# Layer 1 of a two-layer transformer: the second key heads' projection moves behind the first query pairs, the attention's slot table opens earlier, and its prologue runs by a finer clock

## The chip, the cores and the metric

The kernel runs on one core of one Trainium2 chip. The metric is the device time of one execution in microseconds. The kernel before takes 3030.74 us, the median of three runs from 3030.3 to 3031.72.

## The reference

A small diffusion transformer with two layers on 1024 latent tokens and 256 context tokens, model width 1024, 16 heads of 64. Layer 0 mixes by neighbourhood attention, layer 1 by full attention over context and latents with 16 query heads that share 4 key and value heads; both have a gated feed-forward part behind them. The part that matters here is layer 1's mixer:

```python
def qknorm_gqa_mixer(h_lat, h_ctx, w_qkv, q_gain, k_gain, w_o, ang_row, ang_col, with_ctx_out):
    ...
    q, k, v = project_qkv(h_lat, w_qkv, GQA_HEADS, GQA_KV_HEADS)
    qc, kc, vc = project_qkv(h_ctx, w_qkv, GQA_HEADS, GQA_KV_HEADS)
    q = axial_rope(rms_norm(q, q_gain), ang_row, ang_col)
    k = axial_rope(rms_norm(k, k_gain), ang_row, ang_col)
    kc = rms_norm(kc, k_gain)
    k_all = jnp.concatenate([kc, k], axis=1)
    v_all = jnp.concatenate([vc, v], axis=1)
    ...
    def block(q_b):
        s = jnp.einsum('bqhgd,bshd->bhgqs', q_b, k_all).astype(jnp.float32) * scale
        p = jax.nn.softmax(s, axis=-1).astype(v_all.dtype)
        return jnp.einsum('bhgqs,bshd->bqhgd', p, v_all)
    ...
```

## The kernel before, in words

All products are float32 made from two parts, a high and a low one, so that each dense product is three matmuls: high by high (L770), low activations (L771) and low weights (L772). A block of a projection is eight such triples for 512 tokens (24 matmuls of 128x512), or for the 256 context tokens (24 of 128x256); the values have their own three lines (L2105 to L2107).

The stage at hand is layer 1's mixer. Its projections are jobs in one queue of a class Lanes (`bg`): values, queries in pairs of heads (q0 to q7, two heads each, in two blocks of 512 tokens), keys in two pairs: K1d[0] serves the heads 0 to 7, K1d[1] (the job "kv2") the heads 8 to 15. Then comes the output projection. `pump(cost)` gives credit, up to a cap, and emits matmul triples of the first job until it is spent; one triple costs 1. A block that is done is handed to a side generator, finish_qk1, which emits its normalisation and rope: a copy out of PSUM by ScalarE (L2153), a square (L2158), a mean over the head by TensorE (L2162), logarithm and exponential (L2166, L2168), a product on VectorE (L2170), a shuffle (L2176), then on GpSimd or VectorE L2178, L2180 and L2182, the high part on ScalarE (L2188) and the low one (L2190), and the writes to DRAM. A weight tile goes through a similar generator: load, high part (L682), low part (L684).

The prologue before the attention can use four PSUM banks for these blocks (bank1: two S, ps1, X) if the job says so (`prolog`), and temporaries from the set `early` or `late`; in the attention there is one bank, ps1, and `late` has two tiles xn and one each of rs, y, ph and pl. `tick()` moves the emission's own clock by 650 ns, offers each engine's slots to the side generators, and pumps 1. `turn()` moves it by 227 ns, serves only engines that it holds to be idle by their estimated busy time, and pumps a third.

The attention is a list of 64 pairs (16 heads, two blocks of 512 queries, two pairs of 128-query tiles in each). A Plan places the steps of each pair by the table ORDER1 (a name and a time within the pair, in ns, at a period of 8172) and sorts them all by time. X and S are scores (X against the context keys, S against the latent ones, each from two K tiles: L2230, L2231, L2246, L2247), m and mX maxima, e exponentials (L849), s the scaling by the sum on GpSimd (L860), T the transposes (L867), c the copies out of PSUM (L875, L880), PV the product with the values (L497), r and z the output (L895, L907, L908). Between them stand background slots, FILL: PF pumps the projection queue by the phase's rate (1.262), AF, DF and GF offer a slot of ScalarE, VectorE or GpSimd to the side generators, MS and LN the mean and the logarithm. The last three periods have slots without a pair; the first has only its own. head_setup1 loads a head's keys, values and queries into SBUF; it first runs `bg.until` for the head's query block, that is, ticks until that block is finished, and for head 8 until "kv2" is. Its keys' tiles take the memory that the prologue's value tiles (`c`) leave.

Of the kernel before, what the change touches and what calls it, by code (L numbers as in the profile page):

```python
# [25 lines left out]
PAIRS = HEADS // 2  # L26
# [5 lines left out]

V_NMIX, V_NFFN, V_NFIN, V_B, V_QG, V_KG, V_C = 0, 16, 32, 40, 136, 137, 138
V_N = 154
CFG = dict(lag=3, tv=8.0, tm=5.0, t1=43.0, t2=58.0, p0=28, lo="GD", n=39, ra=2.3, rc=0.7, rq=1.1, rb=1.05, gap=263, r1=1.262, lh=300, tk='ADAG', tb=1000000000.0, tg=1, lp='GD')
PERIOD1 = 8172
ORDER1 = {
# [35 lines left out]
def _build(tc, nc, I, O, top):  # L73
    v, s, g, t = nc.vector, nc.scalar, nc.gpsimd, nc.tensor

    def dma(out, in_):
        if out.dtype == F32R:
            out = out.bitcast(F32)
        if in_.dtype == F32R:
            in_ = in_.bitcast(F32)  # L80
        nc.sync.dma_start(out=out, in_=in_)
# [17 lines left out]
    def vec(base, k):  # L99
        return vecs[:, base + k:base + k + 1]  # L100
# [127 lines left out]
    K1d = [dram.tile([2, P, LAT + CTX], F32R, name=f"K1d{p}") for p in range(2)]  # L228
# [38 lines left out]
    def startup():  # L267

        ET = mybir.EngineType
        with ExitStack() as ph:  # L270
# [10 lines left out]
            def start(at, gen):  # L281

                heapq.heappush(todo, (at, next(count), gen))
# [9 lines left out]
            def load_raw(k, src):  # L293
                raws[k] = wraw.tile([P, D], F32, name="wr")
                if k[0] == "v":
                    dma(out=raws[k][:].rearrange("p (u n) -> p u n", u=2), in_=src.rearrange("u p n -> p u n"))
                else:
                    dma(out=raws[k][:], in_=src)

            def loads():  # L300
                W = I["wqkv0"]
                for m in range(KC):
                    load_aw(m)
                    yield 2.9
                    if m < 2:
                        load_x(0, m)
                        yield 2.9
                    if m in (2, 4):
                        k = "k" if m == 2 else "q"
                        load_raw(k, W[8 if m == 2 else 0])  # L310
                        start(now + 3.5, split(k, wsp))
                        yield 1.5
                for i in range(2):
                    load_raw(f"v{i}", W[16:18, :, i * 512:i * 512 + 512])
                    start(now + CFG["tv"], split(f"v{i}", w0))
                    yield 1.5
                for i in range(2):
                    load_x(1, i)
                    yield 2.9
                xs.append(tmp.tile([P, KC, 256], F32, name="aw", bufs=3))  # L320
                load_x(2, 0, 1)
                yield 2.9
                for w in range(2):
                    dma(out=Cd[w], in_=crow[w][:])
                    yield 1.5
                for m in (1, 9):
                    load_raw(f"u{m}", W[m])
                    yield 1.5
                for _ in bias_steps():
                    yield 0.7  # L330

            def split(k, pool):
                hi = pool.tile([P, D], F32R, name="wh")
                lo = pool.tile([P, D], F32R, name="wl")
                ws[k] = hi, lo
                s.copy(hi[:], raws[k][:])
                yield 1.2
                v.tensor_tensor(lo[:], raws[k][:], hi[:].bitcast(F32), ALU.subtract)  # L338
# [16 lines left out]
            def stat(b):  # L355
                n = BLK[b][1]
                acc = []
                for kc in range(KC):
# [10 lines left out]
                    yield 0.55  # L369
                yield CFG["tm"] if b == 1 else 2.0  # L370
                ms = psp.tile([P, 512], F32, name="ms")
# [65 lines left out]
            def first_qk(b):  # L437
# [3 lines left out]
                for kc in range(KC):  # L441
                    while (b, kc) not in ready or b == 0 and min(kc + CFG["lag"], KC - 1) not in ready:
                        yield 0.2
# [20 lines left out]

            for at, gen in [(0.0, loads()), (5.0, c_rows()), (10.0, stat(0)), (CFG["t1"], stat(1)), (CFG["t2"], stat(2)), (28.0, projections())] + \
                    [(max(9.5, a), modulation(m)) for m, a in enumerate((7.0, 13.0, 18.7, 23.0, 26.0, 30.4, 33.3, 36.2))]:
# [32 lines left out]
    class Ring:  # L499

        def __init__(self, n):
            self.n, self.k, self.back = n, 0, set()
# [41 lines left out]
    class Lanes:  # L544
# [145 lines left out]
            self.rings[job.dst].give(job.ids[i])  # L690

        def pump(self, cost):
            self.credit = min(self.credit + cost, self.cap)
            while self.main and self.credit > 0:
                job = self.main[0]
                if len(job.ws) < job.need:
                    break
                try:
                    r = next(job.gen)
                except StopIteration:  # L700
                    self.main.pop(0)
                    if job.heir is not None:
                        job.heir.ws, job.heir.ids, job.heir.dst = job.ws, job.ids, job.dst
                    else:
                        for i in range(len(job.ids)):
                            self.release(job, i)
                    continue
                if isinstance(r, float):
                    self.credit -= r
                elif r == "wait":  # L710
                    break
                else:
                    self.enter(job.tag, r, 1500)

        def tick(self, cost=1.0):

            self.now += 650
            for e in "TML" + CFG["tk"]:
                if self.busy.get(e, 0) < self.now + CFG["tg" if e == "G" else "tb"]:
                    self.slot(e)  # L720
# [12 lines left out]
    def unit(name, k):  # L733
        return [lambda raw: dma(out=raw[:], in_=I[name][k])]
# [177 lines left out]
    class Plan:  # L912
# [1 line left out]
        FILL = ("PF0", "PF1", "PF2", "AF0", "AF1", "AF2", "AF3", "DF0", "DF1", "DF2", "DF3",  # L914
                "DF4", "GF0", "GF1", "GF2", "MS", "LN")

        def __init__(self, phases):

            self.steps, t0 = [], 0
            for k, (period, order, pairs, rate, gap) in enumerate(phases):  # L920
                extra = 3 if k == len(phases) - 1 else 0
                for name, at in order.items():
                    for j in range(len(pairs) + extra * (name in self.FILL)):
                        self.steps.append((t0 + at + j * period, name, pairs[j] if j < len(pairs) else None, rate))
                t0 += len(pairs) * period + gap
            self.steps.sort(key=lambda x: x[0])
# [93 lines left out]
    class Ffn:  # L1020
# [208 lines left out]
        def more(self):  # L1229

            self.ring.idle += self.again()
            if self.layer == 0:
                self.raws.idle += self.xrs + self.tmp[3:]
                self.S.idle += self.tmp[:3]
                self.outs.idle += self.Tf
                self.raws.leave(self.early.idle, self.prepared)
            else:
                self.raws.idle += self.xrs
                self.S.idle += self.Tf
                self.outs.idle += self.tmp  # L1240
# [539 lines left out]
    with ExitStack() as ph:  # L1780
# [6 lines left out]
        bg = Lanes(pb)  # L1787
# [239 lines left out]
        for i, job in enumerate(bg.main[:2]):  # L2027
# [4 lines left out]
        pairs = [[Pair0(h, ps, i) for h in range(HEADS) for i in range(3 - ps)] for ps in range(2)]  # L2032
        n = CFG["n"]
        plan = Plan([(PERIODA, ORDERA, pairs[0][:n], CFG["ra"], 0), (PERIODA, ORDERA, pairs[0][n:], CFG["rq"], CFG["gap"]),
                     (PERIODB, ORDERB, pairs[1], CFG["rb"], 0)])
# [23 lines left out]
    kg = vec(V_KG, 0)  # L2059
# [3 lines left out]
    busy_banks = set()  # L2063
# [19 lines left out]
    def proj_qk1(dst, gain, blks, temps=None, prolog=False):  # L2083

        def gen(job):
            for b in blks:
                n = BLK[b][1]
                while b not in normed:
                    yield "wait"
                k, ps = yield from bank(prolog)  # L2090
                yield from dense_steps(ps[:, :n], job.ws[0], *acts[b], n)
                yield finish_qk1(ps, dst, gain, b, temps or late, k)
        return gen
# [46 lines left out]
    late = Counted(xn=2, sq=2, rs=1, y=1, ph=1, pl=1)  # L2140
# [282 lines left out]
    def add_q(p, blks, *opts):  # L2423
        bg.add((p, blks[0]), unit("wqkv1", p), proj_qk1(Q1d[p], lambda: qg[:], blks, *opts))
# [14 lines left out]
    add_q(0, (0,), early, True)  # L2439
    bg.add("kv", unit("wqkv1", 8), proj_qk1(K1d[0], lambda: kg, (0, 1, 2), early, True))  # L2440
    bg.add("kv", halves("wqkv1", 10), proj_v1((4, 5, 6, 7, 8, 9)))
    bg.add("kv2", unit("wqkv1", 9), proj_qk1(K1d[1], lambda: kg, (2, 0, 1), late, True))
    add_q(1, (0,), late, True)
    for p in range(2, PAIRS):
        add_q(p, (0,))
    for p in range(PAIRS):
        add_q(p, (1,))
# [13 lines left out]
    live["open"] = True  # L2461
    bg.lo, bg.cap = CFG["lp"], 6.0
    pairs = [Pair1(h, b) for blk in range(2) for h in range(HEADS) for b in (4 * blk, 4 * blk + 2)]
    plan = Plan([(PERIOD1, ORDER1, pairs, CFG["r1"], 0)])
    while bg.pending("kv", (0, 0), "norm1"):
        bg.tick()
    h0.close()
    pb = l1.enter_context(tc.tile_pool(name="pg", bufs=2, reuse_waits="tile"))
    head_setup1(0, 0)
    bg.lo, bg.cap = "D", 3.0  # L2470
    def more():
        return any(job.tag == (1, 0) for job in bg.main)

    while busy_banks - {("ps1", 0)} or more():
        bg.tick(float(more()))
    bg.enter("o0", out_split(0))
    bg.enter("o1", out_split(1))
    live["att"] = True
# [159 lines left out]
```

## Time and profile before

| what | us |
|---|---|
| median of three runs | 3030.74 |
| profiled execution, its own time | 3030.41 |
| its span in the trace | 3028.6 |
| lowest and highest of the three | 3030.3, 3031.72 |

The page gives each engine's busy time and its share of the span; a matmul's duration in a timeline overlaps the next one's, so that the distance of two starts is the time that one costs. "Granted clock" is the share of full speed that TensorE was given. In a list of waits, "PE X L2230 <- ACT Pt L849" reads: TensorE's instruction of line 2230 stood idle until ScalarE's at line 849 was done. The prediction quotes the lines that it uses.

### The profile page before, as it was taken

Reading aid. Unit: us, or ns where it says so; the run is one execution under the profiler, and the core shown is the slowest. Engines: PE = TensorE matmul, PEld = TensorE weight load, DVE = VectorE, ACT = ScalarE, POOL = GpSimd, SP = SyncE. Lnnn points to the kernel's source line nnn. Section 1 sums busy time; section 2 is a strip of 40 time slices with the busy share of each in tenths; the row PEclk is TensorE's granted clock in tenths of the full one; section 3 lists DMA queues with packets and bytes.
Section 4 is the critical chain, followed back from the end, with each engine's and each line's share of the span. In section 5 each row is a group of like instructions: output and inputs, shape, how many; then the busy total and the mean of one; then the engine's idle time right before and its main releaser. Section 6 shows DMA issues by size and latency. Waiting matters only on the chain.

```text
span 3028.6 us, 50110 instructions
## 1 busy us (share of the span) xinstructions
PE 2917.2 (96%) x16460; PEld 2503.2 (83%) x16460; DVE 2304.4 (76%) x4659; ACT 1621.8 (54%) x3739; POOL 1245.6 (41%) x1109
## 2 busy tenths in 40 slices
PE   7999998899999999999999899999999999999998
PEld 4788997788788888888889788888888878888886
DVE  7588778776698785557777588899887887776776
ACT  4345545766652222224456488898887632333444
POOL 4246556766234451121121256666643344223112
PEclk9999999999999999999999999999999999999999
DMA  7777777787535562239656523333323443224962
GB/s 265 218 228 242 225 223 226 226 233 207 201 129 195 195 225 85 96 127 330 213 190 215 167 86 93 100 102 105 111 73 122 139 139 118 105 105 147 325 216 108
DMA packets 307170, 519.03 MB, mean 171 GB/s; under 512 B 46432, under 2 KB 112096, under 8 KB 305120
## 3 DMA queue, kind: packets, MB, share of 16 engines
q1 hardware_dynamic: 306912, 515.84, 52.6%
q8 instruction: 131, 2.15, 0.3%
q14 instruction: 127, 1.04, 0.1%
HBM read 389.61 MB, written 120.18 MB: 168 GB/s over the span
## 4 chain that ended last, share of the span: by engine, by line
PE 77%; DVE 9%; DMA 5%; ACT 3%; POOL 3%; issue 2%; SPq 1%; DVEq 0%; POOLq 0%; ACTq 0%
PE pf L1461 9%; PE pf L1462 9%; PE pf L1463 9%; PE T L867 5%; PE o L497 5%; PE pf L1711 5%; PE pf L1710 5%; PE pf L1709 5%; PE ps L770 3%; PE ps L771 3%; PE ps L772 3%; DMA K<-Kd 2%; PE S L2246 2%; PE S L2247 2%; DVE pT L880 1%
## 5 line engine op out<-in xcount | busy, mean ns | idle before, releaser
L860 POOL TENSOR_SCALAR Pt<-Pt,rc 128x1280 f32<-128x1280 f32 (+3 forms) x288 | 299.4, 1040 | 389.0 <-ACT pT L875 143.8
L875 ACT CAST pT<-T 128x256 fp32r<-128x256 f32 (+2 forms) x672 | 305.0, 477 | 124.7 <-PE T L867 120.1
L880 DVE TENSOR_TENSOR pT<-T,pT 128x256 fp32r<-128x256 f32 (+2 forms) x672 | 341.7, 534 | 31.2 <-ACT pT L875 30.8
L867 PE MATMUL T<-ident,Pt 128*128 128x128 f32 x1952 | 302.5, 274 | 23.8 <-POOL Pt L860 22.9
L867 PEld LDWEIGHTS T<-ident,Pt 128*128 128x128 f32 x1952 | 235.2, 140 | 79.6 <-POOL Pt L860 35.4
L497 PE MATMUL o<-pT,Vt 128*128 128x256 f32 x1952 | 295.6, 290 | 2.3 <-DVE pT L880 2.2
L770 PE MATMUL ps<-ah,wh 128*128 128x512 f32 (+1 forms) x688 | 261.3, 380 | 5.5 <-ACT ah L432 2.6
L497 PEld LDWEIGHTS o<-pT,Vt 128*128 128x128 f32 x1952 | 254.3, 189 | 9.5 <-DVE pT L880 5.7
L771 PE MATMUL ps<-al,wh 128*128 128x512 f32 (+1 forms) x688 | 251.5, 366 | 5.3 <-POOL al L132 3.6
L849 ACT ACTIVATE Pt<-S,rc 128x512 f32<-128x512 f32 (+2 forms) x384 | 247.4, 654 | 9.6 <-DVE rc L841 6.5
L772 PE MATMUL ps<-ah,wl 128*128 128x512 f32 (+1 forms) x688 | 250.9, 365 | 1.4 <-DVE wl L338 1.4
L2238 DVE TENSOR_REDUCE nm<-S 128x1 f32<-128x512 f32 x256 | 169.6, 682 | 35.8 <-PE S L2247 34.1
L952 POOL TENSOR_TENSOR c<-c,c 128x512 f32<-128x512 f32 (+1 forms) x63 | 92.6, 1472 | 248.7 <-DVE c L955 89.5
L955 DVE TENSOR_TENSOR c<-c,c 128x512 fp32r<-128x512 f32 (+1 forms) x166 | 131.3, 804 | 48.5 <-ACT c L1437 34.6
L849 ACT ACTIVATE Pt<-X,rc 128x256 f32<-128x256 f32 x256 | 125.2, 489 | 65.3 <-DVE rc L841 58.6
L1437 ACT CAST wh<-c 128x512 fp32r<-128x512 f32 x112 | 68.9, 618 | 166.9 <-PE pf L1462 66.8
L895 POOL TENSOR_TENSOR r<-ob 128x256 f32<-128x256 f32 x144 | 123.7, 859 | 65.4 <-ACT ob L889 58.7
L772 PEld LDWEIGHTS ps<-ah,wl 128*128 128x128 f32 x688 | 131.1, 191 | 23.3 <-DVE wl L338 2.1
L771 PEld LDWEIGHTS ps<-al,wh 128*128 128x128 f32 x688 | 132.0, 192 | 18.5 <-POOL al L132 5.2
L770 PEld LDWEIGHTS ps<-ah,wh 128*128 128x128 f32 x688 | 131.5, 191 | 18.6 <-ACT ah L432 2.8
L1461 PE MATMUL pf<-c,wh 128*128 128x512 f32 x376 | 146.5, 390 | 0.0
L1462 PE MATMUL pf<-c,wh 128*128 128x512 f32 x376 | 146.5, 390 | 0.0
(599 smaller groups left out, 9155.3 us busy)
## 6 DMA issues: line engine op xcount, KB each, us to landing
c<-in_fout SPq DMA_DIRECT2D x119, 256.0 KB, 4.0
wr<-in_wqkv SPq DMA_DIRECT2D x53, 512.0 KB, 4.2
wr<-in_adaT SPq DMA_DIRECT2D x96, 256.0 KB, 3.2
c<-in_fin SPq DMA_DIRECT2D x68, 256.0 KB, 2.9
adaw<-in_adaT SPq DMA_DIRECT2D x64, 256.0 KB, 4.0
wr<-in_wo SPq DMA_DIRECT2D x32, 512.0 KB, 4.5
wr<-in_fin SPq DMA_DIRECT2D x58, 256.0 KB, 2.7
K<-Kd SPq DMA_DIRECT2D x64, 224.0 KB, 4.6
```

What stands on the lines that cost most here:

```text
L497: t.matmul(o_ap, lhsT=u.V[:, kb, :], rhs=u.pT[:, i, :], start=i == 0, stop=i == len(u.blocks) - 1)
L770: t.matmul(ps, lhsT=hi[:, c], rhs=ah[:, kc, :n], start=kc == 0, stop=False)
L771: t.matmul(ps, lhsT=hi[:, c], rhs=al[:, kc, :n], start=False, stop=False)
L772: t.matmul(ps, lhsT=lo[:, c], rhs=ah[:, kc, :n], start=False, stop=kc == KC - 1)
L849: s.activation(u.Pt[:, off:off + u.wid[c]], u.S[c], AF.Exp, bias=u.min, scale=u.sign, accum_out=u.rc[:, 3 + c:4 + c])
L860: g.tensor_scalar(Pt, Pt, u.rc[:, 2:3], 1.0, ALU.mult, ALU.mult)
L867: t.transpose(T[:, i * P:(i + 1) * P], u.Pt[:, (i0 + i) * P:(i0 + i + 1) * P], ident[:])
L875: s.copy(u.pT[:, i0:i0 + n, :P], u.T[c])
L880: v.tensor_tensor(u.pT[:, i0:i0 + n, P:], u.T[c], u.pT[:, i0:i0 + n, :P].bitcast(F32), ALU.subtract)
L1461: t.matmul(ps[:], lhsT=r32(hi[:, c]), rhs=bh, start=k == 0, stop=False)
L1462: t.matmul(ps[:], lhsT=r32(hi[:, c]), rhs=bl, start=False, stop=False)
L1463: t.matmul(ps[:], lhsT=r32(lo[:, c]), rhs=bh, start=False, stop=k == 3)
```

## The change

Six edits, all in what sets the order around layer 1's prologue and attention:

1. the job "kv2" goes behind q1 and q2 in the queue, and it and q1 no longer take the prologue's banks (they are given the default, one bank, and the set `late`);
2. the prologue's loop runs `turn()` in place of `tick()`; behind it, a loop that ticked until every bank but one was free and q1 done is replaced by 24 turns;
3. Plan gets a last argument: if it is given, FILL slots of six periods ahead of the first pair, from 1400 ns before the start on, are added without a pair at that rate (4.0);
4. the first two pairs form a phase of their own with rate 3.0;
5. the rate of the other pairs goes from 1.262 to 1.31;
6. a single pump may bring as much credit as its cost, even above the cap of 3.

Below line 917 a line of the kernel before stands 7 lines further down in the changed one (L2162 is L2169 there, L2230 is L2237).

```diff
@@ -32,7 +32,7 @@
 
 V_NMIX, V_NFFN, V_NFIN, V_B, V_QG, V_KG, V_C = 0, 16, 32, 40, 136, 137, 138
 V_N = 154
-CFG = dict(lag=3, tv=8.0, tm=5.0, t1=43.0, t2=58.0, p0=28, lo="GD", n=39, ra=2.3, rc=0.7, rq=1.1, rb=1.05, gap=263, r1=1.262, lh=300, tk='ADAG', tb=1000000000.0, tg=1, lp='GD')
+CFG = dict(lag=3, tv=8.0, tm=5.0, t1=43.0, t2=58.0, p0=28, lo="GD", n=39, ra=2.3, rc=0.7, rq=1.1, rb=1.05, gap=263, r1=1.31, lh=300, tk='ADAG', tb=1000000000.0, tg=1, lp='GD')
 PERIOD1 = 8172
 ORDER1 = {
     "PF0": -1360, "X": -660, "GF0": -582, "S00": 0, "mX": 30, "S10": 868, "m00": 930, "m10": 1550, "mn0": 2370,
@@ -690,7 +690,7 @@
             self.rings[job.dst].give(job.ids[i])
 
         def pump(self, cost):
-            self.credit = min(self.credit + cost, self.cap)
+            self.credit = min(self.credit + cost, max(self.cap, cost))
             while self.main and self.credit > 0:
                 job = self.main[0]
                 if len(job.ws) < job.need:
@@ -914,9 +914,16 @@
         FILL = ("PF0", "PF1", "PF2", "AF0", "AF1", "AF2", "AF3", "DF0", "DF1", "DF2", "DF3",
                 "DF4", "GF0", "GF1", "GF2", "MS", "LN")
 
-        def __init__(self, phases):
+        def __init__(self, phases, ramp=0.0):
+
 
             self.steps, t0 = [], 0
+            period, order, pairs, rate, gap = phases[0]
+            for name in self.FILL if ramp else ():
+                for j in range(-6, 0):
+                    at = order.get(name, -1e9) + j * period
+                    if at >= -1400:
+                        self.steps.append((at, name, None, ramp))
             for k, (period, order, pairs, rate, gap) in enumerate(phases):
                 extra = 3 if k == len(phases) - 1 else 0
                 for name, at in order.items():
@@ -2439,9 +2446,10 @@
     add_q(0, (0,), early, True)
     bg.add("kv", unit("wqkv1", 8), proj_qk1(K1d[0], lambda: kg, (0, 1, 2), early, True))
     bg.add("kv", halves("wqkv1", 10), proj_v1((4, 5, 6, 7, 8, 9)))
-    bg.add("kv2", unit("wqkv1", 9), proj_qk1(K1d[1], lambda: kg, (2, 0, 1), late, True))
-    add_q(1, (0,), late, True)
-    for p in range(2, PAIRS):
+    add_q(1, (0,))
+    add_q(2, (0,))
+    bg.add("kv2", unit("wqkv1", 9), proj_qk1(K1d[1], lambda: kg, (2, 0, 1)))
+    for p in range(3, PAIRS):
         add_q(p, (0,))
     for p in range(PAIRS):
         add_q(p, (1,))
@@ -2461,18 +2469,15 @@
     live["open"] = True
     bg.lo, bg.cap = CFG["lp"], 6.0
     pairs = [Pair1(h, b) for blk in range(2) for h in range(HEADS) for b in (4 * blk, 4 * blk + 2)]
-    plan = Plan([(PERIOD1, ORDER1, pairs, CFG["r1"], 0)])
+    plan = Plan([(PERIOD1, ORDER1, pairs[:2], 3.0, 0), (PERIOD1, ORDER1, pairs[2:], CFG["r1"], 0)], 4.0)
     while bg.pending("kv", (0, 0), "norm1"):
-        bg.tick()
+        bg.turn()
     h0.close()
     pb = l1.enter_context(tc.tile_pool(name="pg", bufs=2, reuse_waits="tile"))
     head_setup1(0, 0)
     bg.lo, bg.cap = "D", 3.0
-    def more():
-        return any(job.tag == (1, 0) for job in bg.main)
-
-    while busy_banks - {("ps1", 0)} or more():
-        bg.tick(float(more()))
+    for _ in range(24):
+        bg.turn()
     bg.enter("o0", out_split(0))
     bg.enter("o1", out_split(1))
     live["att"] = True
```

## The prediction

> **What bounds the kernel now.** I read the page's first part, then the table of stretches around the second layer's projections, then TensorE's waits, then the timeline of TensorE and of SyncE's queue at the first attention step. First the page, with each engine's busy time:
>
> ```profile
> span 3028.6 us, 50110 instructions
> PE 2917.2 (96%) x16460; PEld 2503.2 (83%) x16460; DVE 2304.4 (76%) x4659; ACT 1621.8 (54%) x3739; POOL 1245.6 (41%) x1109
> ```
>
> TensorE is the bound and the change leaves its instructions as many as they were, so only its idle time and its clock can move. The span is 1.81 us under the profiled execution's own 3030.41 us, which is 0.33 us under the median of 3030.74. Next some stretches (columns: stretch, length, busy time of PE, its weight loads, DVE, ACT and POOL, granted clock, DMA share, GB/s):
>
> ```profile
> 1600.00:1650.00 50.00, 48.07 (x385) 46.50 (x384) 44.27 (x74) 33.95 (x62) 4.31 (x3) 1.00 0.70 237
> 1650.00:1700.00 50.00, 47.02 (x305) 41.86 (x304) 26.36 (x46) 22.64 (x47) 13.65 (x13) 1.00 0.39 125
> 1690.00:1700.00 10.00, 10.00 (x86) 10.00 (x85) 2.97 (x7) 2.26 (x5) 0.00 (x0) 1.00 0.52 170
> 1710.00:1715.00 5.00, 5.00 (x24) 4.13 (x23) 0.91 (x2) 2.20 (x5) 0.00 (x0) 1.00 1.02 265
> 1725.00:1743.00 18.00, 11.54 (x49) 7.66 (x49) 13.33 (x27) 10.63 (x29) 5.80 (x4) 0.81 0.52 164
> 1800.00:1900.00 100.00, 99.79 (x664) 87.46 (x663) 86.61 (x203) 89.25 (x234) 65.86 (x59) 1.00 0.38 111
> 2600.00:2700.00 100.00, 100.00 (x443) 82.81 (x442) 71.85 (x97) 31.88 (x53) 28.92 (x21) 1.00 0.31 109
> ```
>
> The running attention (1800 to 1900) is 99.8% full: a projection moved into it is not hidden, it costs its TensorE time. That time is 100/443 = 0.226 us for a 128x512 matmul, and 10/86 = 0.116 us for a 128x256 one. The hole is the attention's opening, 1725 to 1743, with 11.5 of 18 us busy at a clock of 0.81. Its waits, and below them those of the rest of that attention half (wanted: total us, times, longest):
>
> ```profile
> PE S L2246 <- ACT xn L2153: 2.9, 1, 2.9
> PE S L2246 <- ACT Pt L849: 2.6, 2, 1.8
> PE S L772 <- DVE wl L684: 1.3, 1, 1.3
> PE ps L770 <- ACT xn L2153: 1.0, 1, 1.0
> PE T L2162 <- DVE pT L880: 1.0, 1, 1.0
> PE T L867 <- POOL Pt L860: 0.4, 1, 0.4
> PE X L2230 <- ACT Pt L849: 0.4, 1, 0.4
> ...
> PE S L2246 <- DVE pT L880: 3.2, 8, 0.7
> ```
>
> **The opening, step by step.** TensorE's rows from the first matmul behind the values' projection to the first product of weights and values (columns: start, duration, operation, and the idle time before it):
>
> ```profile
> 1700.05 0.28 PE L770 MATMUL S<-ah,wh 128*128 128x256 f32 x1
> 1701.73 0.39 PE L772 MATMUL S<-ah,wl 128*128 128x256 f32 x1 [1.28 <-DVE wl L684]
> ...
> 1725.05 0.28 PE L2230 MATMUL X<-K,Qs 128*128 128x256 f32 x1
> 1729.01 0.80 PE L2246 MATMUL S<-K,Qs 128*128 128x512 f32 x1 [2.85 <-ACT xn L2153]
> 1732.01 0.80 PE L2246 MATMUL S<-K,Qs 128*128 128x512 f32 x1 [1.78 <-ACT Pt L849]
> 1734.74 0.63 PE L772 MATMUL ps<-ah,wl 128*128 128x512 f32 x1
> 1735.79 0.39 PE L2230 MATMUL X<-K,Qs 128*128 128x256 f32 x1 [0.41 <-ACT Pt L849]
> 1736.99 0.44 PE L867 MATMUL T<-ident,Pt 128*128 128x128 f32 x2 [0.45 <-POOL Pt L860]
> 1743.08 1.42 PE L497 MATMUL o<-pT,Vt 128*128 128x256 f32 x10
> ```
>
> The waits sum to 1.28+2.85+1.78+0.41+0.45 = 6.8, and the 0.96 on L880 (the list's 1.0) makes 7.7. Seven matmuls from 1732.01 to 1735.17 took 3.16 us, not 7 x 0.226 = 1.58: 1.6 lost to the clock. The two from 1729.01 lost 0.6. The opening of before thus loses 9.9 us.
>
> Now TensorE's order from the last value matmul (S<-wl at L2107) to the first transposes of attention weights (L867); X and S<-K are scores, ps and S<-ah projections. Before:
>
> ```order
> L2107 MATMUL S<-wl,ah_17871 128x256
> L770 MATMUL S<-ah_17871,wh 128x256
> ...
> L770 MATMUL S<-ah_17390,wh 128x512
> ...
> L2162 MATMUL T<-sq,hones 128x512
> ...
> L770 MATMUL ps_18448<-ah_17390,wh 128x512
> L771 MATMUL ps_18448<-al_17391,wh 128x512
> L772 MATMUL ps_18448<-ah_17390,wl 128x512
> L2230 MATMUL X<-K_18280,Qs 128x256
> L2231 MATMUL X<-K_18281,Qs 128x256
> ```
>
> and after, at the same place:
>
> ```order
> L2114 MATMUL S<-wl,ah_17854 128x256
> L770 MATMUL ps_18295<-ah_17390,wh 128x512
> ...
> L2238 MATMUL X<-K_18279,Qs 128x256
> L2253 MATMUL S<-K_18278,Qs 128x512
> L2254 MATMUL S<-K_18279,Qs 128x512
> L770 MATMUL ps_18352<-ah_17390,wh 128x512
> ...
> L2169 MATMUL T<-sq,hones 128x512
> L2253 MATMUL S<-K_18278,Qs 128x512
> ```
>
> Before X stood 24 matmuls of 0.116 and 81 of 0.226 (21 us, the second key heads and one query pair); now 24 of 0.226 remain, 5.4 us. Behind the first four scores now come 12 projection matmuls, then four scores, then 9 more: 21 x 0.226 = 4.7 us and a mean-square (L2169) fill what was idle. But X needs keys and queries from DRAM. SyncE's queue at that place (start, time on the queue, transfer):
>
> ```profile
> 1701.11 0.36 SPq L81 DMA_DIRECT2D V1d<-c  x1
> 1703.59 2.39 SPq L81 DMA_DIRECT2D K<-K1d  x4
> 1706.70 1.09 SPq L81 DMA_DIRECT2D Qs<-Q1d  x2
> ```
>
> and the landing of two of them (KB each, us from issue to landing):
>
> ```profile
> Qs<-Q1d SPq DMA_DIRECT2D x2, 128.0 KB, 9.1
> V1d<-c SPq DMA_DIRECT2D x1, 256.0 KB, 2.3
> ```
>
> The last V1d write landed at 1701.11+2.3 = 1703.4 and the K loads, whose tile reuses its cells, were issued at 1703.59. The queries landed 9.1 us after 1706.7 to 1707.8, that is 1715.8 to 1716.9: 15.8 to 16.9 us after the values' end. The queue's order, before and after:
>
> ```order
> L81 DMA V1d<-c_17794 128x4x128
> L81 DMA wr<-in_wqkv 128x1024
> L81 DMA K_18280<-K1d_133 64x1280 x2
> L81 DMA K_18281<-K1d_133 64x1280 x2
> L81 DMA Vt<-V1d 128x1280
> L81 DMA Qs<-Q1d_125 64x512 x2
> ```
>
> ```order
> L81 DMA V1d<-c_17792 128x4x128
> L81 DMA wr<-in_wqkv 128x1024 x2
> L81 DMA K_18278<-K1d_133 64x1280 x2
> L81 DMA K_18279<-K1d_133 64x1280 x2
> L81 DMA Vt<-V1d 128x1280
> L81 DMA Qs<-Q1d_125 64x512 x4
> ```
>
> A second weight tile (wr, 512 KB) now stands ahead of the keys; at the 265 GB/s of the full stretch it is 2.0 us. So X waits between 15.8-5.4 = 10.4 and 16.9+2.0-5.4 = 13.5 us; I take 12, where before it waited for nothing. TensorE behind it is in order: nothing else starts. The clock then starts low. The row above needed 3.2 us of work to come back, at a loss of 1.6; I take that (the bounds are 0 and the 2.2 that the old opening lost). The Trainium skill (TensorE: Matmul & The Clock Gate, Part 1: The HAM clock gate) says that the clock halves after an idle window of about 3.4 us and comes back after about 3.4 us of sustained work; here it had halved by the end of an idle stretch of only 2.85 us, and the return agrees. By its figure the loss would be half of 3.4, an estimate of 1.7 in place of 1.6.
>
> Of the inner waits I keep 0.3 at the scores and 0.8 at L880. The new opening loses 12+1.6+0.3+0.8 = 14.7 against 9.9: +4.8. The two 50 us stretches ahead of it idle 1.9+3.0 us; the prologue by the clock puts the weights' low halves ahead of the values' copies, so I give it one 1.2 us wait back (0 to 4.9). Net +3.6, from 0 to +7.
>
> **GpSimd and head 6.** The rope of a key or query block in the attention costs GpSimd four operations, beside the scaling L860 that each transpose group waits for (counts and mean ns in the groups by line):
>
> ```profile
> L860 POOL TENSOR_SCALAR Pt<-Pt,rc 128x1280 f32<-128x1280 f32 x128 | 172.2, 1346 | 228.2 <-ACT pT L875 141.1 <-DVE rc L841 50.3 <-DVE rc L855 18.2
> L2182 POOL TENSOR_TENSOR xn<-xn,y 128x512 f32<-128x512 f32 x16 | 25.8, 1612 | 0.1
> L2180 POOL TENSOR_TENSOR y<-y,rope 128x512 f32<-128x512 f32 x15 | 24.2, 1612 | 0.0
> L2178 POOL TENSOR_TENSOR xn<-xn,rope 128x512 f32<-128x512 f32 x17 | 23.5, 1380 | 38.3 <-DVE y L2176 38.3
> L2190 POOL TENSOR_TENSOR pl<-xn,ph 128x512 fp32r<-128x512 f32 x16 | 22.4, 1399 | 2.9 <-ACT ph L2188 2.9
> ```
>
> A block is 1.38+1.61+1.61+1.40 = 6.0 us of GpSimd. With the second keys queued ahead of the third query pair, head 6 finds its queries unfinished: head_setup1's bg.until runs the background there until they are ready, and pushes out the rest of one block and two whole ones. GpSimd's order between the same two scalings (the 21st and 22nd of the attention), before and after (r is an output, z its sum):
>
> ```order
> L860 TENSOR_SCALAR Pt<-Pt,rc 128x1280
> L2180 TENSOR_TENSOR y<-y,rope 128x512
> L907 TENSOR_TENSOR z<-z,r 64x256
> L908 TENSOR_TENSOR z<-z,r 64x256
> L860 TENSOR_SCALAR Pt<-Pt,rc 128x1280
> ```
>
> ```order
> L860 TENSOR_SCALAR Pt<-Pt,rc 128x1280
> L2197 TENSOR_TENSOR pl<-xn,ph 128x512
> L2185 TENSOR_TENSOR xn<-xn,rope 128x512
> L2187 TENSOR_TENSOR y<-y,rope 128x512
> L2189 TENSOR_TENSOR xn<-xn,y 128x512
> L2197 TENSOR_TENSOR pl<-xn,ph 128x512
> L2185 TENSOR_TENSOR xn<-xn,rope 128x512
> L2187 TENSOR_TENSOR y<-y,rope 128x512
> L2189 TENSOR_TENSOR xn<-xn,y 128x512
> L2185 TENSOR_TENSOR xn<-xn,rope 128x512
> L2197 TENSOR_TENSOR pl<-xn,ph 128x512
> L2187 TENSOR_TENSOR y<-y,rope 128x512
> ```
>
> Eleven rope operations, about 16.4 us, stand where one stood. TensorE meanwhile has 54 projection matmuls, 12.2 us, and its usual pair beside them, so the sum of work nearly balances; but it can't run ahead. Projections have one PSUM bank (ps1) here, freed by an ACT copy into one of two xn tiles, and an xn tile comes free only at L2197 of two blocks earlier. I follow the chain: the first block change waits for a rope tail, ACT's exponentials and the copy (about 2), the second for the mean-square's return, rope and L2197 of the block before (about 3), and the pair behind it for ACT, which stands at the third copy (about 1.5). That makes 6.5 if no link overlaps, 2 if only the copies show; the one block change of before that shows such a wait cost 1.0 (ps L770 on xn). I take 5.
>
> At the second pair a smaller pile of five rope operations (7.6 us) now stands between two scalings, with some 6 us of TensorE work beside it: +2, against the 1.0 and 0.4 of before: +0.6 (-1 to +2). The higher rate r1 leaves three instead of six pairs of the half without a projection to fill them; the 3.2 us at L880 in eight waits are theirs, and half of it goes: -1.5 (-3 to 0). The queries of heads 2 and 3 are now loaded behind z's transfer on SyncE, and the last pairs have fewer fillers: +0.7 (0 to +3). The wider cap of the credit only lets the new rates of 3 and 4 through, and is in the order above.
>
> **Sum.** 3.6+5+0.6-1.5+0.7 = +8.4 on 3030.41, 3038.8; with the 0.33 of the median, 3039.1, say 3039.
>
> **Rivals.** (1) Not slower: the burst at head 6 is hidden, since GpSimd's 16.4 us lie beside 12.2 us of projections and a pair of some 7 us. For it: GpSimd's work has cover by sum, and the one wait of TensorE for GpSimd in the list of the opening is 0.4. Against: one bank, two xn tiles. It decides if the copies come within 0.5 us of the blocks' ends. It takes the 5 away: 3034. (2) Faster: the transfers ahead of X are short. All four K loads and the queries were issued into a full queue; without it a load takes what the small writes take, 2.3 (V1d), so X is ready 7.7+2.3 = 10 us after the values and waits 4.6, not 12. With a clock that stays up (-1.6), the prologue's whole 4.9 us given back (-3.7 more) and head 6's burst hidden, 8.4-7.4-1.6-3.7-5 = -9.3: 3021. Against it: the queue is full by this very set of transfers. (3) Worse: the chain at head 6 is serial for each of three blocks, 3 us apiece as in the second step, 9 in place of 5: +12.4, 3043. It decides if rope, tail and copy of a block run one behind the other with ACT's exponentials between them. (4) That the slots of missing pairs pump nothing is excluded by the order above, where their 12 and 9 matmuls stand.
>
> **How the numbers follow.** A measurement of this kernel can tell about 0.2%, 6.1 us: same is 3024.7 to 3036.8. My forecast (3036 to 3042) has 0.45, rival 3 has 0.17, rival 1 0.28, rival 2 0.10. Of the forecast's own spread 0.06 falls under 3036.8. Slower is 0.45-0.06+0.17 = 0.56, same 0.28+0.06 = 0.34, faster 0.10. The range leaves out rival 2 and the far half of rival 3: 3028 to 3046.
>
> **What would show it.** Right: TensorE idle 10 to 13.5 us ahead of the first X with its releaser a DMA of K or Qs; a clock of about 0.5 for the 3 us behind it; TensorE full between the first scores and the first transposes; at head 6 waits of projections on xn summing to some 5 us. Wrong: an X that waits under 7 us, or head 6 without a wait over 1 us, or new waits of over 3 us in later pairs, which I have not counted.

## The result, and the profile after

The changed kernel takes 3050.96 us (median of seven runs, 3039.59 to 3056.45) against 3030.74 for the one before (seven runs, 3026.97 to 3036.26): a ratio of 1.0059, 95% interval 1.0041 to 1.0077. It is slower, by 12 to 23 us. The forecast had the direction, not the size: 3039 lay 12 us too low, and 3046, the top of the range, 5 us.

The profiled execution of the changed kernel took 3039.59 us, the shortest of the seven, so its own distance to before (9.2 us) is not the result. Up to the values of layer 1 both kernels have the same instructions. The first matmul of the values and the last group of the program, in the profile of before (start and duration first):

```profile
1644.60 0.33 PE L2105 MATMUL S<-wh,ah 128*128 128x256 f32 x1
...
3015.00 1.88 PE L168 MATMUL pf<-o,ones 128*128 128x512 f32 x4
```

and in that of after:

```profile
1636.93 0.34 PE L2112 MATMUL S<-wh,ah 128*128 128x256 f32 x1
...
3024.19 1.88 PE L168 MATMUL pf<-o,ones 128*128 128x512 f32 x4
```

This execution was 7.7 us ahead when the changed part began. From there to the end it took 1387.26 us, where before took 1370.40: the changed part costs 16.9 us, which fits the timed ratio. A second profile of the changed kernel (below) had its first values at 1646.29, so the lead was not the change's doing. In the eleven profiles of the experiments this point lies between 1641.56 and 1651.32 us.

The waits of TensorE from there to the middle of the next stage, after (total us, times, longest):

```profile
PE X L2237 <- DMA Qs<-Q1d: 11.5, 1, 11.5
PE ps L770 <- ACT xn L2160: 5.3, 3, 2.7
PE S L2253 <- ACT Pt L849: 4.7, 3, 3.3
PE T L867 <- POOL Pt L860: 3.2, 4, 1.0
...
PE pf L190 <- DVE c L144: 2.3, 1, 2.3
PE S L2253 <- DVE pT L880: 2.1, 5, 0.7
...
PE X L2237 <- ACT Pt L849: 1.9, 6, 0.4
PE pf L770 <- ACT ah L2277: 1.3, 1, 1.3
PE T L867 <- DVE pT L880: 0.7, 1, 0.7
...
PE S L772 <- DVE wl L684: 0.2, 1, 0.2
```

Rows of before that are needed beside these and are not in the prediction, from the same stretch:

```profile
PE T L867 <- POOL Pt L860: 2.2, 4, 0.7
PE pf L190 <- DVE c L144: 0.7, 1, 0.7
PE ps L770 <- DVE al L2287: 0.8, 1, 0.8
PE S L772 <- DVE wl L684: 2.3, 2, 1.3
```

The old waits of the opening on xn (2.9) are gone, those on wl are down from 2.3 to 0.2, and one on a transfer, 11.5, has come. Two waits of after, 2.6 on L1444 and 1.9 on L2165, are as long in before. TensorE's rows at that place (the last column is the idle time before), and the clock behind it (stretch, length, busy times of PE, its loads, DVE, ACT, POOL, then the clock):

```profile
1710.08 0.55 PE L2237 MATMUL X<-K,Qs 128*128 128x256 f32 x1 [11.46 <-DMA Qs<-Q1d]
```

```profile
1710.00:1713.00 3.00, 2.92 (x9) 2.56 (x10) 1.39 (x2) 0.00 (x0) 0.00 (x0) 0.50 1.03 244
1713.00:1716.00 3.00, 3.00 (x11) 2.35 (x11) 1.46 (x3) 1.96 (x5) 0.00 (x0) 0.72 1.00 230
1716.00:1722.00 6.00, 5.54 (x26) 4.07 (x25) 3.09 (x9) 3.54 (x11) 1.70 (x1) 1.00 0.23 80
```

The wait is where the prediction put it. Behind it 3.0 us at half clock and 3.0 at 0.72 lose 1.5+0.8 = 2.3 us; then TensorE is 5.54/6 full up to the transposes.

At the place that the prediction calls the second pair (by the trace GpSimd's pile of five between the fifth and the sixth scaling, at 1738.24 and 1747.48) stands a wait of another kind than the one forecast. ScalarE, GpSimd and TensorE there, after (start, duration, operation, idle before):

```profile
1741.34 1.59 POOL L2189 TENSOR_TENSOR xn<-xn,y 128x512 f32<-128x512 f32 x1
1742.96 0.62 ACT L2195 CAST ph<-xn 128x512 fp32r<-128x512 f32 x1 [2.69 <-POOL xn L2189]
1743.48 0.68 ACT L849 ACTIVATE Pt<-S,rc 128x512 f32<-128x512 f32 x1
1744.31 0.50 PE L2253 MATMUL S<-K,Qs 128*128 128x512 f32 x1 [3.31 <-ACT Pt L849]
```

and a stretch a little later:

```profile
1745.00:1750.00 5.00, 5.00 (x24) 4.50 (x23) 2.79 (x6) 3.70 (x10) 4.52 (x5) 0.66 0.27 91
```

ScalarE stands 2.69 us at the rope's high part (L2195), which waits for GpSimd's sum (L2189). The exponential L849 is behind it in ScalarE's queue, and TensorE's next scores need the PSUM bank that it reads: 3.31 us. No scaling L860 is late. Then the clock halves for a while: 5 us at 0.66 lose 1.7 more. The Trainium skill (TensorE: Matmul & The Clock Gate, Part 1, Architectural detail) says that ScalarE and VectorE are strict first-in-first-out; these four rows agree.

At head 6, the two block changes and the end of the burst:

```profile
1819.81 0.50 PE L770 MATMUL ps<-ah,wh 128*128 128x512 f32 x1 [1.51 <-ACT xn L2160]
1829.08 0.50 PE L770 MATMUL ps<-ah,wh 128*128 128x512 f32 x1 [2.67 <-ACT xn L2160]
1838.03 0.50 PE L2253 MATMUL S<-K,Qs 128*128 128x512 f32 x1 [0.70 <-ACT Pt L849]
1841.47 0.50 PE L770 MATMUL ps<-ah,wh 128*128 128x512 f32 x1 [1.09 <-ACT xn L2160]
```

That is 6.0 us, at the block changes that the prediction followed (a block change is the first matmul of a new projection block, which needs the one bank free again).

### The profile page after: what moved, and what is told of

It reads as the page before. It is cut to its first block, busy times and chain, and to the rows that moved or that the text cites. A ratio compares the mean times of both kernels' runs of the same rounds, so it can differ in the third digit from the quotient of the medians.

```text
span 3037.8 us, 50121 instructions
## 1 busy us (share of the span) xinstructions
PE 2918.2 (96%) x16460; PEld 2504.8 (82%) x16460; DVE 2297.6 (76%) x4657; ACT 1622.0 (53%) x3739; POOL 1245.7 (41%) x1109
## 5 line engine op out<-in xcount | busy, mean ns | idle before, releaser
L860 POOL TENSOR_SCALAR Pt<-Pt,rc 128x1280 f32<-128x1280 f32 (+3 forms) x288 | 299.2, 1039 | 438.5 <-ACT pT L875 143.8
L880 DVE TENSOR_TENSOR pT<-T,pT 128x256 fp32r<-128x256 f32 (+2 forms) x672 | 342.3, 535 | 32.8 <-ACT pT L875 31.9
L770 PE MATMUL ps<-ah,wh 128*128 128x512 f32 (+1 forms) x720 | 274.5, 381 | 9.1 <-ACT xn L2160 5.3
L771 PE MATMUL ps<-al,wh 128*128 128x512 f32 (+1 forms) x720 | 263.7, 366 | 3.6 <-POOL al L132 2.4
L772 PE MATMUL ps<-ah,wl 128*128 128x512 f32 (+1 forms) x720 | 263.5, 366 | 1.4 <-DVE wl L338 1.4
L849 ACT ACTIVATE Pt<-S,rc 128x512 f32<-128x512 f32 (+2 forms) x384 | 247.7, 656 | 18.4 <-DVE rc L841 15.8
L849 ACT ACTIVATE Pt<-X,rc 128x256 f32<-128x256 f32 x256 | 125.5, 490 | 65.4 <-DVE rc L841 58.6
L1444 ACT CAST wh<-c 128x512 fp32r<-128x512 f32 x112 | 68.8, 618 | 167.5 <-PE pf L1469 63.6
L770 PEld LDWEIGHTS ps<-ah,wh 128*128 128x128 f32 x720 | 138.3, 192 | 23.8 <-ACT xn L2160 6.3
L772 PEld LDWEIGHTS ps<-ah,wl 128*128 128x128 f32 x720 | 137.4, 191 | 24.5 <-DVE wl L338 2.1
L771 PEld LDWEIGHTS ps<-al,wh 128*128 128x128 f32 x720 | 138.5, 192 | 17.6 <-POOL al L132 4.0
```

The source lines that it names most:

```text
L770: t.matmul(ps, lhsT=hi[:, c], rhs=ah[:, kc, :n], start=kc == 0, stop=False)
L771: t.matmul(ps, lhsT=hi[:, c], rhs=al[:, kc, :n], start=False, stop=False)
L772: t.matmul(ps, lhsT=lo[:, c], rhs=ah[:, kc, :n], start=False, stop=kc == KC - 1)
L849: s.activation(u.Pt[:, off:off + u.wid[c]], u.S[c], AF.Exp, bias=u.min, scale=u.sign, accum_out=u.rc[:, 3 + c:4 + c])
L860: g.tensor_scalar(Pt, Pt, u.rc[:, 2:3], 1.0, ALU.mult, ALU.mult)
L880: v.tensor_tensor(u.pT[:, i0:i0 + n, P:], u.T[c], u.pT[:, i0:i0 + n, :P].bitcast(F32), ALU.subtract)
```

## The experiments

Theory: the move of the second key heads costs 17 us, by the cover that X loses and by the two piles of rope work; the rest of the change is about neutral. Rivals: the run-to-run clock behind the new wait makes the result; the second key heads cost more wherever in the attention they stand; the other edits cost by themselves. Ratios are to the kernel before on the same chip, with 95% intervals. "Stretch" is the time from the first matmul of the values to the last group in the profile (before 1370.40, after 1387.26).

### The changed kernel again

No edit.

> The changed kernel itself, once more. Theory: in its first profile the stages ahead of layer 1's projections, whose instructions are the same in both kernels, were 7 us shorter than in the profile of before, by chance of the granted clock; the changed stages cost 17 us: 12 to 13 of wait at the first X, the rest in the piles of rope operations at the second pair and at head 6. So 14 to 20 us above before here, with an X wait of 11 to 12 us and 7 to 8 us of projection waits at head 6. Rival: only 10 us are the changed stages, and what runs have above that is half clock behind the new wait; then this profile shows at least 7 us more of half clock in the opening than the first one did (13.7 us).

3051.42 us, ratio 1.0060 (1.0047 to 1.0073), stretch 1389.46. Its waits that differ from the first profile's, or would have to:

```profile
PE X L2237 <- DMA Qs<-Q1d: 14.0, 1, 14.0
PE ps L770 <- ACT xn L2160: 5.3, 3, 2.7
PE S L2253 <- ACT Pt L849: 4.6, 3, 3.3
```

and the stretches from X on:

```profile
1720.00:1723.00 3.00, 2.52 (x8) 2.26 (x9) 1.13 (x2) 0.00 (x0) 0.00 (x0) 0.50 1.04 231
1723.00:1726.00 3.00, 3.00 (x13) 2.46 (x13) 1.72 (x4) 1.67 (x5) 0.00 (x0) 0.92 1.02 201
```

The waits in the list are the same to 0.1 us, but for L2277 (1.6 for 1.3) and X: 14.0 us, 2.5 more than in the first profile and above my bound of 13.5. The projection waits sum to 5.3, under the 7 to 8 expected. Behind X (at 1720.48) TensorE ran at half clock for 2.5 us and at 0.92 for 3.0, which loses 1.3+0.2 = 1.5, less than the 2.3 of the first time. The rival by the clock falls: the span is 11.6 us longer than the first (3049.4, 3037.8); 9.4 of that lie ahead of the changed part and 2.5 at X.

### The move alone

The kernel before with one edit:

```diff
-    bg.add("kv2", unit("wqkv1", 9), proj_qk1(K1d[1], lambda: kg, (2, 0, 1), late, True))
-    add_q(1, (0,), late, True)
-    for p in range(2, PAIRS):
+    add_q(1, (0,))
+    add_q(2, (0,))
+    bg.add("kv2", unit("wqkv1", 9), proj_qk1(K1d[1], lambda: kg, (2, 0, 1)))
+    for p in range(3, PAIRS):
         add_q(p, (0,))
```

> The kernel before with one edit alone: the second key heads go behind q1 and q2, and both lose the prologue's banks. 24 projection matmuls stand ahead of the first X, none behind it until the first product with the values, and a burst of 57 at head 6. Theory: an X wait of 11 to 12, the 8 us behind X idle as before, 8 at head 6: before +18 to +24, so the move by itself costs as much as the whole change or more. Rival, that the prologue by turns, the slots ahead of the first pair or the higher rates carry a good part: under +12.

3052.27, ratio 1.0072 (1.0058 to 1.0087), that is +18 to +26; stretch 1396.05. From its opening and head 6:

```profile
PE X L2230 <- DMA Qs<-Q1d: 8.7, 1, 8.7
PE ps L770 <- ACT xn L2153: 8.6, 3, 5.0
```

The move by itself costs about what the whole change does. Its X wait is shorter than I expected, its block changes longer: the 8.6 are 1.0 in the opening and two of the three waits on xn at head 6, where with the third (1.1, behind the end of this list) and 0.7 on L849 TensorE stands 9.4 us.

### Everything but the move

The changed kernel with "kv2" and q1 back in front with their banks, in place of the 24 turns the loop on busy_banks and more() with `bg.turn()`:

```diff
...
+    bg.add("kv2", unit("wqkv1", 9), proj_qk1(K1d[1], lambda: kg, (2, 0, 1), late, True))
+    add_q(1, (0,), late, True)
...
-    for _ in range(24):
-        bg.turn()
...
+    while busy_banks - {("ps1", 0)} or more():
         bg.turn()
```

> The changed kernel with the second key heads and q1 back in front with the prologue's banks, and the loop ahead of the attention waiting for them as before, by turns. Theory: the cover of the loads is back, no burst at head 6; the chain behind the first scores has 6 fillers and a mean-square instead of 21 matmuls: before -3 to +3. Rival (prologue by turns or the higher rates cost something by themselves): over 5 us above before.

3036.23, ratio 1.0009 (1.0000 to 1.0019), stretch 1373.99: 3.6 more than before, 13 less than the changed kernel. No wait on a transfer is left in its list of 1690 to 1800 us; new is one of 2.7 on xn. So most of the loss is the move's; the other edits gain nothing.

### More cover ahead of X

```diff
-    for _ in range(24):
+    for _ in range(100):
```

> 100 turns in place of 24 ahead of the attention, nothing else: the order then has q1, q2 and a part of the second key heads ahead of the first X (63 matmuls of 128x512 and 24 of 128x256), the fillers behind it stay, and no burst is left at head 6. Theory: the X wait of 11.6 goes to under 1, the 8 us at head 6 go, about 3 us less at the second pair: 17 below the changed kernel, that is before -3 to +2 us. Rival, that the second key heads cost more in the attention wherever they are put: most of them are still in it, so over 10 us above before.

3034.68, ratio 1.0012 (1.0001 to 1.0022), stretch 1377.39. In the opening:

```profile
PE ps L770 <- ACT xn L2160: 6.4, 4, 3.2
PE S L2253 <- DVE pT L880: 1.2, 2, 0.9
PE S L2253 <- ACT Pt L849: 0.7, 1, 0.7
```

No X wait and no burst, by one number; some 15 of 18 us come back (ratio 1.0060 to 1.0012). The rival's bar, over 10 us above before, is not reached. But the trace has 72 matmuls of 128x512 and 24 of 128x256 ahead of X, more than I had counted: two of the three blocks of the second key heads stand there and only one is left in the attention. What all three would cost there with a full cover ahead of X, this run does not show. What is left are waits at block changes, three ahead of X (1.1, 1.0, 3.2) and one behind it (1.0): ahead of X too, the jobs now have one bank and two xn tiles.

### The prologue's banks for q1 and q2, 120 turns

```diff
-    add_q(1, (0,))
-    add_q(2, (0,))
+    add_q(1, (0,), late, True)
+    add_q(2, (0,), late, True)
...
-    for _ in range(24):
+    for _ in range(120):
```

> The changed kernel with 120 turns ahead of the attention and the prologue's banks for q1 and q2: 96 matmuls of 128x512 and 24 of 128x256 ahead of X, 12 with a mean-square and 9 behind the first scores, no burst at head 6. Theory: no X wait, under 2 us of the 6.4 us of bank waits of the run with 100 turns, the chain behind X filled: before -6 to 0. Rival: the second key heads in one bank keep 4 to 6 us of waits: +1 to +5.

3034.85, ratio 1.0009 (0.9999 to 1.0020), stretch 1372.33. The block changes on xn still wait 5.7 us (two, longest 3.2): the rival's case. Both stand ahead of X, between blocks of the second key heads, which have the one bank.

### q3 ahead of the second key heads

```diff
-    add_q(1, (0,))
-    add_q(2, (0,))
+    for p in (1, 2, 3):
+        add_q(p, (0,))
     bg.add("kv2", unit("wqkv1", 9), proj_qk1(K1d[1], lambda: kg, (2, 0, 1)))
-    for p in range(3, PAIRS):
+    for p in range(4, PAIRS):
```

> The changed kernel with q3 ahead of the second key heads too. The opening is the same, the burst of 54 projection matmuls at head 6 is gone, and one of 39 stands at head 8. Theory: the X wait stays 11 to 12; head 6 gives 8 us back, head 8 takes about 5: before +11 to +16. Rival (clock behind the X wait is the cost): as the changed kernel, before +15 to +20.

3055.15, ratio 1.0075 (1.0063 to 1.0088), that is +19 to +27; stretch 1391.48. It is no better than the changed kernel (1.0047 to 1.0073), against both expectations. Waits before and after 1800 us:

```profile
PE X L2237 <- DMA Qs<-Q1d: 12.3, 1, 12.3
...
PE ps L770 <- DVE al L2294: 6.7, 1, 6.7
PE S L2253 <- DVE pT L880: 4.6, 10, 0.8
PE ps L770 <- ACT xn L2160: 1.7, 1, 1.7
```

The waits on xn fell from 5.3 to 2.8 (this 1.7 and 1.1 in the opening), as the theory of head 6 has it; the 1.7 and 0.7 on L849 belong to a burst of 39 projection matmuls at head 8, half of the 5 that I had given it. But a wait of 6.7 us came at the end. The addition L2294, which frees the bank, stands in VectorE's order behind L2279, and that waits for the last heads' results to come back from DRAM, with no other projection queued. That the work pulled forward is what is missing there fits, but no run here separates it.

### The rope's tail on VectorE too

```diff
-            yield "D" if tp is early else "G" if live["att"] else "GD"
+            yield "D" if tp is early else "G" if live["att"] and not bg.pending("kv2") else "GD"
```

> The changed kernel in which the last three rope operations of a block may go to VectorE too, as long as the second key heads are not done (in the attention they are GpSimd's alone). Theory: at the second pair and at head 6 ScalarE stands in order behind GpSimd's rope chain, and TensorE behind ScalarE; with a shorter chain 4 to 8 of these 11 us go: before +10 to +15, the X wait stays. Rival, that the single bank and the two xn tiles alone make the waits at head 6: no change from the changed kernel, before +16 to +20.

3046.69, ratio 1.0046 (1.0032 to 1.0061): some 4 us less than the changed kernel's second measurement, the intervals overlapping; stretch 1389.65, no shorter.

```profile
PE X L2237 <- DMA K<-K1d: 14.0, 1, 14.0
PE ps L770 <- ACT xn L2160: 6.0, 4, 3.3
PE S L2253 <- ACT Pt L849: 1.3, 2, 0.7
```

The four waits on xn, one by one:

```profile
1750.46 0.59 PE L770 MATMUL ps<-ah,wh 128*128 128x512 f32 x1 [3.27 <-ACT xn L2160]
1829.26 0.50 PE L770 MATMUL ps<-ah,wh 128*128 128x512 f32 x1 [0.98 <-ACT xn L2160]
1836.63 0.50 PE L770 MATMUL ps<-ah,wh 128*128 128x512 f32 x1 [0.76 <-ACT xn L2160]
1848.91 0.50 PE L770 MATMUL ps<-ah,wh 128*128 128x512 f32 x1 [1.01 <-ACT xn L2160]
```

The waits of scores on L849 fell from 4.7 to 1.3 (1.9 with one behind 1850 us), longest 0.7 (3.3 in the changed kernel): the second pair's wait was ScalarE behind GpSimd's rope. But nothing is won there, since a block change at the same place now waits 3.3 on its xn tile. At head 6 the three waits on xn fell from 5.3 to 2.8, and 0.7 on L849 stays: of the 6.0 us there, GpSimd's rope made 2.5, and 3.5 stand without it. So theory and rival each hold in part. The stretch is that of the second profile of the changed kernel (1389.46), which has the same X wait; what head 6 gives up is mostly met by waits of 0.7 on L880 and 0.5 on a load of queries that have come elsewhere.

### One weight tile ahead of the key loads

The loader is held to the first two jobs while the last values' job runs (self.hold starts False and is cleared behind head_setup1):

```diff
-                for job in self.main[:4]:
+                for job in self.main[:2 if self.hold else 4]:
...
     while bg.pending("kv", (0, 0), "norm1"):
+        bg.hold = sum(job.tag == "kv" for job in bg.main) <= 1
         bg.turn()
```

> The changed kernel with the weight loader held to the first two jobs while the last values' job runs, so that one weight tile instead of two stands ahead of the key loads in SyncE's queue (and 12 matmuls come later, behind the second X). Theory: the second tile is 512 KB at some 250 GB/s, 2 us: an X wait of 9.5 to 12 in place of 11.6 to 14.2, but the hole behind X is open again by 2 to 3 us: the changed kernel -3 to +2, before +15 to +20. Rival, that the wait is set by the landing of the last V1d write and not by what is queued: X wait as before, 11.5 to 14.

3046.18, ratio 1.0047 (1.0033 to 1.0061), stretch 1382.81.

```profile
PE X L2237 <- DMA Qs<-Q1d: 9.7, 1, 9.7
```

The wait is 1.8 to 4.3 us shorter than in the two profiles of the changed kernel; the second tile's 2.0 us is the right order. From the last value matmul to X it is 15.4 us here and 15.8 in the move alone, which also has one tile there; in the four profiles with two tiles (the changed kernel twice, q3 first, the rope's tail) it is 17.2 to 19.8. So what is queued has a part in the wait, and the rival falls. The second pair's 3.3 us are not there either (0.8 on L849 and 0.5 on xn), which I had not expected: that wait, too, moves with the order of the fillers.

### The slots alone, at two rates and without the first phase

Three kernels with before's queue and loops. First the slots ahead of the first pair, the two pairs at rate 3, the wider credit and r1=1.31:

```diff
-    plan = Plan([(PERIOD1, ORDER1, pairs, CFG["r1"], 0)])
+    plan = Plan([(PERIOD1, ORDER1, pairs[:2], 3.0, 0), (PERIOD1, ORDER1, pairs[2:], CFG["r1"], 0)], 4.0)
```

> The changed kernel with the move and both loops by turns undone: what is left are the slots ahead of the first pair, the phase of two pairs at rate 3, the rate 1.31 and the wider credit. 24 matmuls of 128x256 and 84 of 128x512 stand ahead of X, 12 and a mean-square behind the first scores. Theory: no X wait, half or more of the 8.1 us behind X goes, no burst: before -6 to -1. Rival, that these edits cost by themselves: +2 to +6, as in the run that put only the key heads back.

3033.42, ratio 1.0003 (0.9991 to 1.0015), stretch 1370.52. Then the same at r1=1.262:

> The kernel before with the slots ahead of the first pair, the two pairs at rate 3 and the wider credit, at the old rate of 1.262 (the run before this with 1.31 had 3.6 us less idle behind X, and 3.2 us more at the end, where the output projection waited 3.9 us on L2277). Theory: the queue of projections now lasts to the end, that wait goes under 1: before -5 to -1. Rival, that what is saved behind X comes back wherever the projections run out: before -1 to +3.

3034.19, ratio 1.0009 (0.9997 to 1.0021), stretch 1373.74. Then `Plan([(PERIOD1, ORDER1, pairs, CFG["r1"], 0)], 4.0)` at 1.262:

> The kernel before with the slots ahead of the first pair (and the credit that they need) alone; all pairs at 1.262. 12 matmuls, a mean-square and 3 more stand behind the first scores. Theory: as the run at the old rate, before -5 to -1, since those slots are what fills the hole behind X. Rival: the two pairs at rate 3 do it, so before -1 to +2.

3033.29, ratio 1.0006 (0.9994 to 1.0017), stretch 1370.43. None of the three gains what I expected. The first, in its opening and then at its end:

```profile
PE S L2253 <- ACT xn L2160: 2.2, 1, 2.2
PE X L2237 <- ACT Pt L849: 1.8, 1, 1.8
PE S L2253 <- ACT Pt L849: 0.8, 1, 0.8
...
PE pf L770 <- ACT ah L2277: 3.9, 1, 3.9
```

Behind X its scores wait 2.2+0.8 where those of before wait 2.9+2.6; of this the second X takes 1.8 (before 0.4), and a score waits 1.5 on L880. But at the end stands 3.9 on L2277 where before had 0.8 on L2287. I read that as a fixed store of cover: what fills the hole at the start is missing at the end. At the old rate that wait is 2.0, with 2.3 on L190 (0.7 before), and with the slots alone 1.5: smaller, not gone, so the rate has a part in it. The differences among the three are within their intervals.

## Why the prediction was wrong

The direction and its cause held: the cover of X's loads goes and a wait on the queries takes its place; the move alone makes the loss. The size did not. On equal ground, from the values to the end, I summed 8.4 and the trace shows 16.9 (19.1 in the second profile).

| term | predicted | measured in the profile of after |
|---|---|---|
| new opening: wait, clock, inner waits | 14.7 | 11.5+2.3+0.5 on L860 = 14.3 (12 for X predicted) |
| minus the old opening | 9.9 | 9.9 |
| prologue | -1.2 | wl: 2.3, less the 1.3 in the old opening, to 0.2: -0.8 |
| head 6 | 5 | 6.0 |
| second pair | +0.6 | 3.3+1.7 of clock, less the old 1.0 on xn: +4.0 |
| pairs without fillers | -1.5 | 3.2 to 2.1: -1.1 |
| transposes on L860 | in the above | 2.2 to 3.2: +1.0 (0.5 of each is in the openings too and cancels) |
| late queries and the end | +0.7 | L190 +1.6, L2277 1.3 for L2287 0.8: +2.1 |
| sum | 8.4 | 15.6 of 16.9; of the rest 0.7 is the transposes' wait on L880, and the remainder is not placed |

The step that failed most is "a smaller pile of five rope operations (7.6 us) now stands between two scalings", valued at +0.6. I compared GpSimd's pile with TensorE's work beside it and asked when the next scaling L860 would come. The operation that came late was the exponential, held up in ScalarE's queue by the rope's own L2195; and the wait cost clock on top. I had used that chain for head 6 and not here. It is a sign of being wrong that I had named, a new wait of over 3 us in a later pair. With the rope shortened, one bank and two xn tiles cost the same 3.3 us there, so the place had two such chains and I had priced neither. The second step is the end: I gave it 0.7 by the count of fillers in the last pairs, and it took 2.1; three experiments that bring projections forward show waits of 2.0 to 6.7 us there, while the one with 120 turns has none on the attention's results. How much comes back at the end is open. Head 6 was 1 too low.

That the opening came out within 0.4 of the forecast is partly luck: in the next execution X waited 2.5 us longer.

Rival 1, that head 6's burst is hidden, is out by 6.0 us of waits. Rival 2, short transfers ahead of X, is out: 11.5, 12.3 and 14.0 us. Rival 3 came nearest, with 12.4 of the 16.9, but not for its reason: head 6 took 6.0, not 9 (9.4 only in the move alone). The X wait itself went over my bound, 14.0 against 13.5, in the second profile: I had bounded it by one landing time in one execution.

The range did not fail by the spread of the runs. Single executions lie far apart: twenty-three runs of before beside the first experiments lay between 3026.91 and 3040.7, and the instructions ahead of the change, the same in all kernels, ended 14 us apart over the profiles (1636.93 to 1651.32). But the medians repeat: 3030.41 to 3032.73 for before in four measurements, 3050.96 and 3051.42 for the changed kernel. The spread only says that one profiled execution, such as the 3039.59 here, can't be set against a forecast.

The clock term was assumed from one row, 3.2 us to come back. From X on it took 4.6 us in the first profile (0.65 between 1714 and 1715) and 3.0 in the second. The Trainium skill (TensorE: Matmul & The Clock Gate, Part 1: The HAM clock gate) says that the window over which the clock is set runs freely, so that the return varies with its phase; the two profiles agree with that, the experiments can't show the phase itself.

## What to carry to other kernels

A projection that looks movable may be the cover of a load: before moving it, look for the next instruction that waits on DRAM, and count the work left between the last write that the load needs and that instruction. Where rope or normalisation is spread over engines, follow the in-order queue of the engine that also makes the exponentials; a pile on GpSimd can hurt through it, before its sum of work exceeds TensorE's; and where blocks share one bank and two tiles, look at that chain too, since taking the first wait away can leave the second. Background work is a fixed store: before filling a hole at the start, see what the end will run on.

## What the runs showed of the hardware that was not expected

The clock dropped while TensorE was at work again: after the 3.31 us wait that ended at 1744.31, the stretch from 1745 to 1750 ran at 0.66 with TensorE 5.00 of 5 busy. And the wait for the same queue of loads varied by 2.5 us between two executions of one kernel (X waits 11.5 and 14.0).
